# Cutting the tail's output stores differently, and issuing the very last piece from ScalarE's queue

## The chip, the cores and the metric

The kernel runs on one core of a Trainium2 chip. The metric is device time in microseconds (us), the median of several executions. Between two runs of one kernel the time varies by about 0.1 to 0.3%, so questions of half a per cent are asked here with five rounds, each beside a run of the kernel before on the same chip. A ratio given below is the mean time of one kernel's fast runs over the mean of the other's from the same rounds, so it is not quite the ratio of the quoted medians.

A few words used throughout. A *store* is a DMA from on-chip memory to HBM. *Issue* is the moment when a sequencer hands the store over. The store then runs on 16 DMA engines, each moving its own rows, one *packet* per row here. Each engine reports when its share has *landed*; the store is complete with the last of these reports.

## The reference

```python
batch, m, k, n = 16, 512, 1024, 768
return (np.matmul(x, weight) + bias + residual).astype(np.float32)
```

All inputs and the output are float32. The core reads about 62 MB and writes 25 MB.

## The kernel before

The 8192 rows are worked on as 64 tiles of 128 rows, grouped by J = 8 into super tiles (index S). One partition holds 8 consecutive rows, so a super tile's load or store moves long contiguous rows. A tile's matmuls go in two column chunks, 512 and 256 wide. All large transfers are issued from the sync queue:

```python
def store(S, j0=0, j1=J, n0=0, nl=N):
    K_(nc.sync.dma_start(
        out=out_d[S, :, j0:j1, n0:n0 + nl], in_=ro[S][:, j0:j1, n0:n0 + nl]
    ))
```

`K_` keeps the order of the program on each engine. `finish(t)` is the VectorE add that takes tile t's product out of PSUM and writes the result row, which the store then reads. The tail of the program:

```python
for t in range(HEAD, n_t):
    # ... cast, loads, matmuls, transposes, adds cut ...
    if S == n_s - 1 and j == 0:
        store(S - 1)                    # 3072 KB
    if S == n_s - 1 and j == J // 2:
        store(S, 0, J // 2)             # tiles 0-3: 1536 KB
    if S == n_s - 1 and j == J - 1:
        store(S, J // 2, j)             # tiles 4-6: 1152 KB
t, S = n_t - 1, n_s - 1
for b, (n0, nl) in enumerate(chunks):   # the last tile, chunk by chunk
    po[t] = psum_o(t + b)
    for i in range(len(steps)):
        mm(t, i, n0, nl)
    finish(t, n0, nl)
    store(S, J - 1, J, n0, nl)          # 256 KB, then 128 KB
```

## Time and profile before

The median was 211.06 us (210.88 to 211.19, 3 runs).

| what | value | read from |
|---|---|---|
| span | 209.1 us | page |
| TensorE (PE) busy | 96% | page, busy table |
| sync DMA queue | 97.8% of 16 engines' time | page, queue table |
| last VectorE add ends | 204.9 us | timeline |
| last store: issue to landing | 3.3 us | list of DMA issues |

First, lines of the page of the kernel before: DMA use in 40 slices of the span (tenths), and two DMA queues (packets, MB, share of 16 engines). The q8 packets are fetches of 16 KB of instructions.

```profile
DMA  6999999999999999999999999999999999999966
q1 hardware_dynamic: 5328, 87.03, 97.8%
q8 instruction: 10, 0.16, 0.3%
```

The engines move data nearly all the time. The tail in the timeline of the kernel before (start us, us, engine, line, operation), from 198 us on:

```profile
200.37 4.06 PE L104 MATMUL po<-w_sb,xt 128*128 128x512 bf16 x24
...
201.94 0.96 DVE L131 TENSOR_TENSOR ro<-po,ro 128x768 f32<-128x768 f32 x1 [0.68 <-PE po L104]
202.93 3.02 SPq L78 DMA_DIRECT2D out_dram<-ro  x3
203.67 1.23 DVE L131 TENSOR_TENSOR ro<-po,ro 128x512 f32<-128x512 f32 x2 [0.77 <-PE po L104]
```

PE ends at 204.4 and VectorE at 204.9. Nothing but stores and the closing barriers is left after that. The first of the three issues of the sync queue (the SPq line merges them) starts when tile 6's add is done. The list of DMA issues of the kernel before (size, us from issue to landing):

```profile
out_dram<-ro SPq DMA_DIRECT2D x1, 1536.0 KB, 10.4
out_dram<-ro SPq DMA_DIRECT2D x1, 1152.0 KB, 4.2
out_dram<-ro SPq DMA_DIRECT2D x1, 256.0 KB, 3.4
out_dram<-ro SPq DMA_DIRECT2D x1, 128.0 KB, 3.3
```

And the windows of the kernel before, 1 us each. Behind the engines' busy times come the granted clock, the DMA share and GB/s:

```profile
core 0: us, PE busy (x) PEld busy (x) DVE busy (x) ACT busy (x) POOL busy (x), PEclk, DMA share, GB/s
201.00:202.00 1.00, 1.00 (x8) 0.60 (x7) 0.32 (x2) 0.00 (x0) 0.00 (x0) 1.00 0.67 283
202.00:203.00 1.00, 1.00 (x7) 0.43 (x5) 0.90 (x1) 0.00 (x0) 0.00 (x0) 1.00 0.32 135
203.00:204.00 1.00, 1.00 (x9) 0.71 (x8) 0.33 (x1) 0.00 (x0) 0.00 (x0) 1.00 0.41 172
204.00:205.00 1.00, 0.43 (x4) 0.14 (x2) 0.78 (x2) 0.00 (x0) 0.00 (x0) 1.00 1.05 442
205.00:206.00 1.00, 0.00 (x0) 0.00 (x0) 0.00 (x0) 0.00 (x0) 0.00 (x0) 1.00 1.01 406
206.00:207.00 1.00, 0.00 (x0) 0.00 (x0) 0.00 (x0) 0.00 (x0) 0.00 (x0) 1.00 0.85 340
207.00:208.00 1.00, 0.00 (x0) 0.00 (x0) 0.00 (x0) 0.00 (x0) 0.00 (x0) 1.00 0.68 238
```

Between 201 and 204 the DMA share falls from 0.67 to 0.32 and 0.41: a hole. The 1152 KB store was issued only at 202.93, and its first packet starts at 203.75. This hole is what the change aims at.

These are the landings of each tail store (first, 14th and 16th of 16, us):

```
kernel before   issued   first    14th    16th
1536 KB         193.91  201.21  203.44  204.30
1152 KB         202.93  206.92  207.07  207.12
 256 KB         204.39  207.57  207.71  207.76
 128 KB         204.92  207.95  208.13  208.18
```

The engines finish the 1536 KB store up to 3.1 us apart. Toward the end of the hole two of them are still at work, and the other fourteen are idle.

### The profile page before, as it was taken

The page shows a single profiled execution, that of the slowest core. Times are in us where ns is not written, and L with a number is a line of the kernel's source. Part 1 is how long each engine was busy: PE and PEld are TensorE (multiplying, and loading weights), DVE is VectorE, ACT ScalarE, POOL GpSimd, SP SyncE. Part 2 cuts the span into 40 slices and gives each one's busy share as a digit, 9 for nine tenths or more (in the row PEclk, how much of TensorE's full clock was granted, in tenths as well). Part 3 has the DMA queues.
Part 4 walks back from the last instruction along what each step waited for, and adds up shares of the span by engine and source line. Part 5 has one row for each costly group of instructions (what it writes and reads, how often), then busy time and mean ns, then how long its engine had stood idle before and what let it go on. Part 6 is the DMA issues. An engine that isn't in the chain of part 4 may idle for free.

```text
span 209.1 us, 3149 instructions
## 1 busy us (share of the span) xinstructions
PE 201.1 (96%) x1274; PEld 130.8 (63%) x1299; DVE 105.0 (50%) x139; ACT 68.0 (33%) x68; POOL 115.6 (55%) x71
## 2 busy tenths in 40 slices
PE   7999999999899999999999999999999999999991
PEld 2556666666566666666666666666666666666660
DVE  0646564455354455445545544554554455446551
ACT  2544315520283054323423252440543234322000
POOL 2000197819936655999499802994069900799000
PEclk9999999999999999999999999999999999999999
DMA  6999999999999999999999999999999999999966
GB/s 229 428 422 432 430 421 438 443 456 407 404 476 420 409 432 412 443 428 434 437 415 459 415 414 447 437 426 418 428 431 443 445 412 421 432 442 423 414 287 273
DMA packets 5344, 87.23 MB, mean 417 GB/s; under 512 B 593, under 2 KB 721, under 8 KB 1618
## 3 DMA queue, kind: packets, MB, share of 16 engines
q1 hardware_dynamic: 5328, 87.03, 97.8%
q8 instruction: 10, 0.16, 0.3%
q14 instruction: 4, 0.03, 0.0%
q10 hardware_dynamic: 2, 0.00, 0.0%
HBM read 61.87 MB, written 25.17 MB: 416 GB/s over the span
## 4 chain that ended last, share of the span: by engine, by line
PE 70%; DMA 25%; issue 1%; ACT 1%; DVE 0%; POOL 0%; ACTq 0%; POOLq 0%
PE po L104 60%; DMA x_tile<-in_x_dram 23%; PE pt L95 10%; DMA tmp<-in_bias_dram 2%; ACT xb L87 1%; DVE ro L131 0%; POOL ident masks.py:197 0%; ACTq L87 0%; POOL tmp L135 0%; POOLq L262 0%
## 5 line engine op out<-in xcount | busy, mean ns | idle before, releaser
L104 PE MATMUL po<-w_sb,xt 128*128 128x512 bf16 (+1 forms) x999 | 175.4, 324 | 1.4
L104 PEld LDWEIGHTS <-xt 128*128 128x128 bf16 x1024 | 100.1, 98 | 59.5 <-DVE xt L99 0.5
L87 ACT CAST xb<-x_tile 128x1024 bf16<-128x1024 f32 x62 | 63.2, 1045 | 115.5 <-PE pt L95 63.2
L121 POOL TENSOR_TENSOR ro<-ro,bias_sb 128x768 f32<-128x768 f32 x40 | 71.2, 1816 | 34.6 <-DMA ro<-in_residual_dram 24.6
L99 DVE COPY xt<-pt 128x512 f32<-128x512 f32 x64 | 44.2, 692 | 88.3 <-PE pt L95 88.2
L121 POOL TENSOR_TENSOR ro<-ro,tmp 128x768 f32<-128x768 f32 x24 | 43.1, 1816 | 42.3 <-DMA ro<-in_residual_dram 25.0
L131 DVE TENSOR_TENSOR ro<-po,ro 128x768 f32<-128x768 f32 (+2 forms) x41 | 38.0, 930 | 2.9 <-PE po L104 2.8
L95 PE MATMUL pt<-ident,xb 128*128 128x128 f32 x256 | 38.6, 274 | 0.7 <-ACT xb L87 0.7
L95 PEld LDWEIGHTS pt<-ident,xb 128*128 128x128 f32 x256 | 30.1, 142 | 9.2 <-ACT xb L87 1.3
L129 DVE TENSOR_TENSOR tmp<-po,bias_sb 128x768 f32<-128x768 f32 x24 | 22.8, 949 | 0.4 <-PE po L104 0.4
L170 PE MATMUL po<-warm 128*128 128x512 bf16 x15 | 6.1, 579 | 1.2 <-DVE warm L156 1.2
L176 ACT CAST w_sb<-ro 128x768 bf16<-128x768 f32 x4 | 3.3, 832 | 4.0 <-DMA ro<-in_weight_dram 4.0
L170 PEld LDWEIGHTS <-warm 128*128 128x128 bf16 x15 | 1.9, 132 | 4.1 <-issue 2.8
L87 DVE CAST xb<-x_tile 128x1024 bf16<-128x1024 f32 x2 | 1.4, 694 | 5.1 <-DMA x_tile<-in_x_dram 5.1
L178 DVE CAST w_sb<-ro 128x768 bf16<-128x768 f32 x4 | 2.2, 556 | 2.2 <-DMA ro<-in_weight_dram 2.2
L161 ACT ACT_TABLE_LOAD x1 | 1.3, 1283 | 2.0 <-POOL ident masks.py:199 2.0
L190 PE MATMUL po<-tmp 128*128 128x512 f32 (+1 forms) x4 | 1.5, 486 | 0.0
L198 DVE COPY bias_sb<-po 128x768 f32<-128x768 f32 x1 | 1.0, 958 | 0.1
L190 PEld LDWEIGHTS po<-tmp 128*128 128x128 f32 x4 | 0.7, 190 | 0.5 <-issue 0.5
L135 POOL MEMSET tmp<- 128x768 f32 x1 | 0.7, 737 | 0.3 <-POOLq L262 0.3
L156 DVE MEMSET warm<- 128x256 uint32 x1 | 0.3, 272 | 0.9 <-PEq L262 0.9
masks.py:199 POOL TENSOR_SCALAR_AFFINE_SELECT ident<-ident 128x128 f32<-128x128 f32 x1 | 0.3, 292 | 0.1
(8 smaller groups left out, 1.0 us busy)
## 6 DMA issues: line engine op xcount, KB each, us to landing
x_tile<-in_x_dram SPq DMA_DIRECT2D x6, 4096.0 KB, 29.4
ro<-in_residual_dram SPq DMA_DIRECT2D x7, 3072.0 KB, 18.0
out_dram<-ro SPq DMA_DIRECT2D x7, 3072.0 KB, 24.9
x_tile<-in_x_dram SPq DMA_DIRECT2D x2, 2048.0 KB, 23.9
x_tile<-in_x_dram SPq DMA_DIRECT2D x3, 1024.0 KB, 8.7
ro<-in_weight_dram SPq DMA_DIRECT2D x4, 768.0 KB, 9.1
ro<-in_residual_dram SPq DMA_DIRECT2D x2, 1536.0 KB, 20.9
out_dram<-ro SPq DMA_DIRECT2D x1, 1536.0 KB, 10.4
```

The costliest lines, as they stand in the source:

```text
L87: K_(copy(out=xb[t], in_=x_sb[t // J][:, t % J, :]))
L95: K_(nc.tensor.transpose(out=pt[:, c, :], in_=pairs[:, c * P:(c + 1) * P], identity=ident))
L99: K_(nc.vector.tensor_copy(out=xt[t], in_=pt))
L104: K_(nc.tensor.matmul(po[t][:, n0:n0 + nl], lhsT=both[:, e, :], rhs=w_sb[:, c, e, n0:n0 + nl], start=(i == 0), stop=(i == len(steps) - 1),))
L121: K_(nc.gpsimd.tensor_add(out=r, in0=r, in1=tmp[t] if t < EARLY else bias_sb))
L129: K_(nc.vector.tensor_add(out=tmp[t], in0=p, in1=bias_sb))
L131: K_(nc.vector.tensor_add(out=row(t, n0, nl), in0=p, in1=row(t, n0, nl)))
L161: K_(nc.scalar.copy(out=warm_a, in_=warm_a))
L170: K_(nc.tensor.matmul(warm_ps[:, 0:512], lhsT=warm[:, 0:P], rhs=warm, start=True, stop=True))
L176: K_(nc.scalar.copy(out=w_sb[:, c, e, :], in_=w_st[:, c, e, :]))
L178: K_(nc.vector.tensor_copy(out=w_sb[:, c, e, :], in_=w_st[:, c, e, :]))
L190: K_(nc.tensor.matmul(bias_ps[:, n0:n0 + nl], lhsT=ones, rhs=bias_row[:, n0:n0 + nl], start=True, stop=True,))
```

## The change

Tiles 4 and 5 shall leave 3 us sooner, so that the hole fills; tile 6 follows alone. The very last piece goes out from ScalarE, which is idle by then, since the sync queue spends 1.02 us on that issue.

```diff
-    def store(S, j0=0, j1=J, n0=0, nl=N):
-        K_(nc.sync.dma_start(
+    def store(S, j0=0, j1=J, n0=0, nl=N, queue=nc.sync):
+        K_(queue.dma_start(
             out=out_d[S, :, j0:j1, n0:n0 + nl], in_=ro[S][:, j0:j1, n0:n0 + nl]
         ))
@@
+        if S == n_s - 1 and j == J - 2:
+            store(S, J // 2, j)
         if S == n_s - 1 and j == J - 1:
-            store(S, J // 2, j)
+            store(S, j - 1, j)
@@
         finish(t, n0, nl)
-        store(S, J - 1, J, n0, nl)
+        store(S, J - 1, J, n0, nl, nc.scalar if b else nc.sync)
```

## The prediction

> **What bounds it.** The page's busy table gives PE 96% of the 209.1 us span, its queue table the sync queue 97.8% of the time of 16 DMA engines. After the last matmul the transfers alone count: in the timeline of the tail PE ends at 204.4, the last VectorE add at 204.9, the last store is issued at 204.92 and lands at 208.2 (issue to landing 3.3 us); then barriers to 209.1. The change can touch only the 3.3 us between the last add and that landing.
>
> **What the change does.** No byte, matmul or add is added or removed. The 1152 KB store of tiles 4 to 6, issued at 202.93 after tile 6's add, becomes 768 KB issued after tile 5's add (ends 199.86, 3 us sooner) and 384 KB at 202.93: one more issue (0.33 us of an idle sequencer). The last 128 KB is issued by ScalarE, idle since about 190; its one earlier issue took 0.49 us, the sync queue's last one 1.02 us.
>
> **The tempting gain.** Issue to first packet took 0.83 us for the 1152 KB (202.93 to 203.75). In the window view the bandwidth falls to nearly zero around 203, because the earlier 1536 KB store has run out on most engines. With 768 KB queued early that hole fills: at about 430 GB/s the 1152 KB would be done at 205.3 rather than 206.65, and the last store could land near 206.8, 1.4 us sooner.
>
> **Why I do not expect it.** The Trainium skill, "DMA: Bandwidth & Descriptors", section "Why a DMA increments its semaphore by 16 and not by 1", says that a store runs on up to 16 engines that finish independently and that only all 16 mean landed. The trace agrees, and the engines are far apart: the 16 landings of the 1536 KB store spread from 201.21 to 204.30. Chaining the packet records into 16 engines, I read their last packets of that store at 200.8 to 203.83; 14 are done by 202.9, two at 203.76 and 203.83. The 1152 KB was ready at 203.75. So the two late engines had no hole: each ran without a gap to its last packet at about 207.7. With the change they still have 203.83 + 8 packets of 6144 B (estimate from that size at the start, 1.86 us) + 8 of 3072 B (estimate 0.95) + 8 of 2048 B (0.65, read) + 8 of 1024 B (0.38, read) = 207.7. The other 14 finish earlier and wait. Late engines' packets took the same 0.46 us per 12288 B when others were idle, so I expect no speed-up from that. The ScalarE queue saves issue time only (same page, "Issuing engines are not separate DMA queues"; no run here shows it yet): the last issue ended at 205.94, and the late engines reach its packets only at 207.3.
>
> Expected gain: 0 to 0.2 us.
>
> **Prediction.** 210.9 us, 8 times in 10 within 210.2 to 211.3. Faster by over 2%: 0.01; within 2%: 0.98; slower: 0.01.
>
> **What would show it.** Right: most of the 16 landings of the 768 KB and 384 KB come early, each store's last trails them by 2 to 3 us; DMA stays busy around 203 but thins out from 205.5 to 207.7; the last landing is again at 208.1 to 208.2; the last add still ends at 204.9.
>
> **What would make it wrong.** If the late engines' lag is not there in the new run (instruction fetches of 16 KB, 0.9 us each, may fall elsewhere), or they speed up alone, the end moves toward 206.8 and the time toward 209.7. If ScalarE's queue starts slowly (its first DMA took 4 us to its first packet, behind loads), the end could slip by up to 1 us.

## The result, and the profile after

The changed kernel took 211.13 us (median of 6, 210.96 to 211.40), the kernel before 211.01 in the same rounds. The ratio is 1.0005, with a 95% interval of 0.9992 to 1.0018: the same time. The profiled run: its span is 209.4 us.

The timeline and the issues of the changed kernel:

```profile
199.90 4.83 SPq L78 DMA_DIRECT2D out_dram<-ro  x3
...
203.67 1.23 DVE L131 TENSOR_TENSOR ro<-po,ro 128x512 f32<-128x512 f32 x2 [0.77 <-PE po L104]
204.98 0.38 ACTq L78 DMA_DIRECT2D out_dram<-ro  x1
```

```profile
out_dram<-ro SPq DMA_DIRECT2D x1, 768.0 KB, 6.5
out_dram<-ro SPq DMA_DIRECT2D x1, 384.0 KB, 4.4
out_dram<-ro SPq DMA_DIRECT2D x1, 256.0 KB, 3.6
out_dram<-ro ACTq DMA_DIRECT2D x1, 128.0 KB, 3.3
```

The 768 KB are issued at 199.90, as intended, and ScalarE's issue takes 0.38 us. Yet the last store still needs 3.3 us from issue to landing. The windows of the changed kernel:

```profile
201.00:202.00 1.00, 1.00 (x8) 0.60 (x7) 0.32 (x2) 0.00 (x0) 0.00 (x0) 1.00 0.97 412
202.00:203.00 1.00, 1.00 (x7) 0.42 (x5) 0.91 (x1) 0.00 (x0) 0.00 (x0) 1.00 0.85 356
203.00:204.00 1.00, 1.00 (x9) 0.71 (x8) 0.33 (x1) 0.00 (x0) 0.00 (x0) 1.00 0.77 320
204.00:205.00 1.00, 0.44 (x5) 0.15 (x2) 0.79 (x2) 0.00 (x0) 0.00 (x0) 1.00 0.87 353
205.00:206.00 1.00, 0.00 (x0) 0.00 (x0) 0.00 (x0) 0.00 (x0) 0.00 (x0) 1.00 0.89 343
206.00:207.00 1.00, 0.00 (x0) 0.00 (x0) 0.00 (x0) 0.00 (x0) 0.00 (x0) 1.00 0.46 166
207.00:208.00 1.00, 0.00 (x0) 0.00 (x0) 0.00 (x0) 0.00 (x0) 0.00 (x0) 1.00 0.11 41
```

The hole is filled: the share is 0.97, 0.85 and 0.77 where it was 0.67, 0.32 and 0.41. But the work does not end sooner. It thins out, to 0.46 and then 0.11, where before all engines stopped together. The landings say who is left:

```
changed kernel  issued   first    14th    16th
1536 KB         193.92  201.23  203.38  204.62
 768 KB         199.90  203.05  205.30  206.44
 384 KB         202.93  205.06  206.24  207.36
 256 KB         204.39  206.24  206.88  207.99
 128 KB         204.98  206.61  207.21  208.33   (the 15th: 208.10)
```

Fourteen engines have landed everything by 207.21, 0.9 us sooner than the 14th landing before. The last two land at 208.10 and 208.33, where the last of before was 208.18. The sync queue's waits at the end, between 198 and 210 us (what for: us in total, times, longest), first before, then after:

```profile
SPq L273 <- DMA out_dram<-ro: 2.1, 3, 1.2
```

```profile
SPq L275 <- DMA out_dram<-ro: 3.6, 1, 3.6
```

After the change the sync queue is done with its issues 1.2 us sooner (at 204.73, before at 205.95, by the SPq lines). It then waits that much longer, for an end that has not moved.

### The profile page after: what moved, and what is told of

Same layout as the page of the kernel before. It is cut to its first block, busy times and chain, and to the rows that moved or that the text cites. A ratio compares the mean times of both kernels' runs of the same rounds, so it can differ in the third digit from the quotient of the medians.

```text
span 209.4 us, 3151 instructions
## 1 busy us (share of the span) xinstructions
PE 200.2 (96%) x1274; PEld 130.5 (62%) x1299; DVE 105.0 (50%) x139; ACT 68.1 (33%) x68; POOL 115.6 (55%) x71
## 4 chain that ended last, share of the span: by engine, by line
PE 70%; DMA 25%; issue 1%; ACT 1%; DVE 0%; POOL 0%; ACTq 0%; POOLq 0%
PE po L104 60%; DMA x_tile<-in_x_dram 23%; PE pt L95 10%; DMA tmp<-in_bias_dram 2%; ACT xb L87 1%; DVE ro L131 0%; POOL ident masks.py:197 0%; ACTq L87 0%; POOL tmp L135 0%; POOLq L264 0%
## 5 line engine op out<-in xcount | busy, mean ns | idle before, releaser
L170 PE MATMUL po<-warm 128*128 128x512 bf16 x15 | 5.3, 520 | 1.2 <-DVE warm L156 1.2
```

What stands on the lines that cost most here:

```text
L170: K_(nc.tensor.matmul(warm_ps[:, 0:512], lhsT=warm[:, 0:P], rhs=warm, start=True, stop=True))
```

## The experiments

**The theory (late engines).** Loads and stores have kept the queue full for most of the run, and two engines lag behind the others. In the kernel before they come to the end of their backlog at 203.76 and 203.83, just when the 1152 KB becomes available (203.75): they never saw the hole. More work offered early only makes the other fourteen finish sooner.
**Rivals.** (a) The split gains something and ScalarE's queue loses it again. (b) The end is bound by fixed latencies after the last add, so nothing done to the queue can matter. (c) The backlog of all engines together hides the gain, not two late ones.

### The two halves of the change alone

The first run keeps only the split:

```diff
-        store(S, J - 1, J, n0, nl, nc.scalar if b else nc.sync)
+        store(S, J - 1, J, n0, nl)
```

> Only the split; the last piece stays on the sync queue. Late-engine theory: the two late DMA engines set the end whoever issues, so the time is that of before and after, within 0.3 us (210.8 to 211.4), and the last landing is again at 208.1 to 208.4. Rival (the split gains, ScalarE's queue loses it again): this one is faster than before by 0.5 us or more.

Measured: 211.27 us against 211.31 for before, ratio 0.9993 (0.9981 to 1.0005). In the profiled run, 14 of 16 landings of the last store were in by 207.42, the last two at 208.85 and 208.97. The sync queue's last issue took 0.33 us here, against 1.02 in the kernel before, so with the split there was little left for ScalarE's queue to save.

The second keeps only the queue (`store(S, J // 2, j)` restored, the split's two lines removed):

> Only the other queue; tiles 4 to 6 stay one store. Late-engine theory: same time within 0.3 us, landings of the last store within 0.3 us of each other as before, because the 1152 KB store starts when even the late engines are done. Rival (ScalarE's queue costs what the split gains): slower than before by 0.5 us or more.

Measured: 211.68 us, ratio 1.0016 (1.0000 to 1.0033). The landings of the last store lie between 208.27 and 208.75, further apart than the 0.3 us expected: one engine's share of the 1536 KB landed only at 205.1, and it still trailed the next by 0.3 us at the end. Rival (a) falls: by its interval the split alone gains at most 0.4 us, where 0.5 or more was asked for. Whether the other queue alone costs the 0.16% is at the edge of what these runs resolve (the interval allows 0 to 0.7 us).

### A level start for the tail

If lateness is the cause, the change must gain once the engines are level. This needs the backlog to run out before the tail's stores. It is done by not loading half of the last super tile's x; the data of an earlier super tile is used instead, so the result is wrong (four tiles), with all matmuls and stores unchanged.

```diff
-            if j0 == 0:
+            if S == n_s - 1:
+                x_sb[S], j0 = x_sb[S - X_BUFS], J // 2
+            elif j0 == 0:
                 x_sb[S] = ring(sb, "x_tile", S, X_BUFS, [P, J, K], FP32)
```

The same edit was made in the kernel before, in the changed kernel, and in the split alone.

> The kernel before with 2 MB less to load (the first half of the last super tile's x is not loaded; the previous contents are used, so four tiles are wrong on purpose). The queue then runs dry some 4 us earlier and all engines are idle before the tail's stores. Late-engine theory: same time as before within 0.4 us (210.6 to 211.4), because the 1152 KB store still starts at about 203.7 and ends at 206.6, and the last store lands at about 208.2. Rival (the tail is bound by queue backlog in total): faster by 1 us or more.

> The changed kernel with the same 2 MB less. Late-engine theory: with the engines level before the tail's stores, the gain that the change was meant for appears: last landing at 206.6 to 206.9, time 1.0 to 1.6 us below the light kernel before (209.4 to 210.1). Rival (the end is bound by fixed latencies after the last add, 3.3 us from issue to landing and then barriers): no difference from the light kernel before, within 0.3 us.

> The split alone on the light queue, the last piece on the sync queue. Late-engine theory: the split brings all of the gain; within 0.3 us of the light changed kernel. Rival (the sync queue's long last issue of 1.02 us matters once the engines are level): 0.4 to 0.7 us slower than the light changed kernel.

Measured, five executions each, beside 211.29 us for the kernel before:

| 2 MB less to load in | median, us | ratio to before (95%) |
|---|---|---|
| the kernel before | 211.23 | 0.9997 (0.9984 to 1.0011) |
| the changed kernel | 209.95 | 0.9935 (0.9923 to 0.9948) |
| the split alone | 209.86 | 0.9931 (0.9918 to 0.9945) |

One execution of the first row, the profiled one, took 763 us. It is left out of its ratio (it still counts in its median). Its trace shows TensorE slow throughout (a 128x512 matmul took 1104 ns on average, against 379 in the run below, with VectorE's adds at 948 ns in both); why is not known.

> The light kernel before once more, only because its first profiled execution took 763 us against 211.2 in the other four: a profile of an ordinary execution. Time 210.8 to 211.6; landings of the last store within 0.3 us of each other, the last at 208.0 to 208.4.

It took 211.19 us. The windows of this light kernel before, and then the last line of its list of DMA issues:

```profile
202.00:203.00 1.00, 1.00 (x6) 0.44 (x5) 0.78 (x1) 0.00 (x0) 0.00 (x0) 1.00 0.00 0
203.00:204.00 1.00, 1.00 (x8) 0.59 (x6) 0.23 (x2) 0.00 (x0) 0.00 (x0) 1.00 0.00 0
206.00:207.00 1.00, 0.00 (x0) 0.00 (x0) 0.00 (x0) 0.00 (x0) 0.00 (x0) 1.00 0.82 338
207.00:208.00 1.00, 0.00 (x0) 0.00 (x0) 0.00 (x0) 0.00 (x0) 0.00 (x0) 0.93 0.96 349
```

```profile
out_dram<-ro SPq DMA_DIRECT2D x1, 128.0 KB, 3.3
```

The same two views of the light changed kernel:

```profile
202.00:203.00 1.00, 1.00 (x6) 0.48 (x5) 0.95 (x1) 0.00 (x0) 0.00 (x0) 1.00 0.74 289
203.00:204.00 1.00, 1.00 (x9) 0.65 (x7) 0.23 (x2) 0.00 (x0) 0.00 (x0) 1.00 0.16 61
206.00:207.00 1.00, 0.00 (x0) 0.00 (x0) 0.00 (x0) 0.00 (x0) 0.00 (x0) 1.00 0.43 143
207.00:208.00 1.00, 0.00 (x0) 0.00 (x0) 0.00 (x0) 0.00 (x0) 0.00 (x0) 0.91 0.00 0
```

```profile
out_dram<-ro ACTq DMA_DIRECT2D x1, 128.0 KB, 1.9
```

And the last line of the list of the light split:

```profile
out_dram<-ro SPq DMA_DIRECT2D x1, 128.0 KB, 1.9
```

Both light kernels have all engines idle in the middle of the tail, so all 16 start level. The light kernel before has gained nothing from 2 MB less work: the hole has only become complete (share 0.00), and the last store still takes 3.3 us. In the light changed kernel the last store takes 1.9 us, and its landings lie between 206.71 and 206.95. This is the 1.3 us that the change was meant to bring (211.23 to 209.95). So the change works as intended once the backlog is gone. Rival (b) falls: the 3.3 us are not fixed. The lighter load takes the backlog from all sixteen engines, so this pair alone does not tell the two late engines from rival (c); the landings above and a comparison of four runs below do. The split brings all of it; with ScalarE's queue or the sync queue the last store takes 1.9 us. The sync queue's last issue, 1.02 us in the kernel before, takes 0.33 us in the light split, as it did in the split alone with the full load.

### Which engines are late

The Trainium skill ("DMA: Bandwidth & Descriptors", section "Why a DMA increments its semaphore by 16 and not by 1") states that a store uses the largest number of engines up to 16 that divides its row count, and the lowest-numbered ones. So a piece cut by partitions into row counts such as 88 (11 engines) can tell where the late ones are. The first attempt cut the last 128 KB into six stores (the edit is shortened here):

```diff
+for rows in (4, 8, 12, 14, 15, 75):
+    K_(nc.scalar.dma_start(out=out_d[S, p0:p0 + rows, ...], in_=ro[S][p0:p0 + rows, ...]))
+    p0 += rows
```

> The changed kernel with the last 128 KB cut by partitions into six stores of 4, 8, 12, 14, 15 and 75 rows, to learn how many engines each uses and whether the late ones are among them. Late-engine theory with the skill's rule for the number of engines: 4, 8, 12, 14, 15 and 15 landings, and in each store the landings of late engines trail the others by 1 to 2.5 us; the store in which the late landings first appear brackets the late engines' numbers. Rival (lateness belongs to the last rows written, not to an engine): all six land together at the end or one after the other in order of issue. Time 0 to 1 us longer than the changed kernel for five more issues.

It took 213.15 us, 2.0 us more than the changed kernel where at most 1 was expected, and its profile cannot place the late engines: more stores in flight made tile 6's store wait for a semaphore of one of the small ones (issued at 206.7, not 202.9), so the late engines had caught up by then. It does show the landings: 4, 8, 12, 14, 15 and 15, as the skill says of the number.

The next cut the 256 KB piece into 2 and 126 rows and the 128 KB into 8 and 120 (ScalarE's queue):

> A cleaner probe: in the changed kernel the 256 KB piece is cut by partitions into 2 and 126 rows, the last 128 KB into 8 and 120 rows. By the skill's rule for the number of engines (lowest-numbered k) these use 2, 14, 8 and 15 engines. Late-engine theory: the late landings, trailing by 1 to 2.5 us, appear only in the stores whose engines include the late ones; two of 16 are late, so the 14-engine store shows two late landings unless a late engine is number 14 or 15, and the 8-engine store shows none, one or two. Rival (lateness belongs to each store's last rows): every store shows its late landings. Time within 0.7 us of the changed kernel.

It took 211.45 us (211.22 for before). The 2-engine store landed at 205.7; the 14-engine store has one very late landing, at 208.22 against 207.4 for the one before it; the 15-engine store also has one (208.56 against 207.9). So one late engine is among numbers 2 to 13, counting from 0. The expectation of the next run takes the other for the sixteenth, since the 15-engine store has only one very late landing. The packet records show otherwise: the engine that finished tile 6's 384 KB last of all (landing 207.61) then moved eight packets of the 15-engine store, until 207.54, and none of the 14-engine store. By the rule it is number 14. Its landing at 207.9 is less late only because it had no share of the 256 KB. The 8-engine store, on ScalarE's own queue, had its last landing at 207.6 and says little: there its single packets may not have waited behind the sync queue's. The third cut therefore put everything on the sync queue, as 8 and 120, then 88 and 40 rows:

> To find the second late engine: the changed kernel with both pieces of the last tile on the sync queue, where an engine takes its packets in order, cut by partitions into 8 and 120 rows (256 KB piece), then 88 and 40 rows (128 KB piece), so 8, 15, 11 and 10 engines. The earlier cut showed one very late landing among 14 engines and one among 15, none among the first 2, so one late engine should be the sixteenth and the other one of numbers 2 to 13. Expected: one very late landing (2 us or more behind) in the 15-engine store; in the 8, 11 and 10-engine stores it appears if the engine's number is below 8, 11 and 10, and then in all larger ones. Rival (lateness follows rows, or is spread anew in each store): the four stores disagree with any single number. Time within 0.7 us of the changed kernel.

It took 211.03 us (211.37 for before, one run each). The 15-engine store had one very late landing, at 208.33, with the next at 207.73. The 8-, 11- and 10-engine stores had none so late: their last came at 206.78 (0.44 us after the second last), 208.00 and 208.17, the last two within 0.02 us of their second last. In the packet records the latest engine ends with its share of the 15-engine store (last packet 208.00) and has none of the 11-engine store, so it is one of 11 to 14. The second latest reads the same way, though its packets are harder to tell from others. With number 14 known from the cut before, the other late engine is then one of 11 to 13, if the two are the same in every build.

### Taking work off the late engines

The next expectation still says 15 where the records say 14. For its cut this makes no difference: both late engines have numbers above 10, so stores on 11 and 10 engines relieve them (the edit is shortened again; p0 starts at 0):

```diff
-            store(S, 0, J // 2)
+            for rows in (96, 22, 10):     # the control: (96, 16, 16)
+                K_(nc.sync.dma_start(out=out_d[S, p0:p0 + rows, 0:J // 2, :],
+                                     in_=ro[S][p0:p0 + rows, 0:J // 2, :]))
+                p0 += rows
```

> A version meant to beat both. The two cuts of the last tile placed the late engines among numbers 11 to 13 and at 15 (counting from 0). The changed kernel with the 1536 KB store of the last super tile's tiles 0 to 3 cut by partitions into 96, 22 and 10 rows: 16, 11 and 10 engines, so engines 0 to 9 move 9 rows of it, engine 10 moves 8, engines 11 to 15 move 6 rather than 8. Late-engine theory: the late engines' lag in the tail shrinks by 2 rows of 12288 B, 0.91 us, the others' grows by 0.46 us; the last landing comes 0.3 to 0.9 us sooner than in the changed kernel and the time is 210.2 to 210.8 where before has 211.1. Rival (the cut or its extra issues, not the relief, matter, or lateness is not tied to those engines): same time as before within 0.2 us.

> Control: the same cut into three stores, but 96, 16 and 16 rows, all on 16 engines, so each engine still moves 8 rows. Late-engine theory: no gain, time of the changed kernel within 0.25 us (210.9 to 211.4). Rival (any cut into three helps): as fast as the 96, 22 and 10 cut.

> The relieving cut (96, 22 and 10 rows) in the kernel before, where tiles 4 to 6 are one store issued at 202.9. Late-engine theory: the late engines finish earlier but then wait for that store's first packet at 203.75 like the others, so no gain: 211.0 to 211.4, last landing at 208.1 to 208.3. Rival (relief helps by itself, the split is not needed): 0.3 us or more faster than before.

| cut of the 1536 KB store | in | median, us | ratio to before (95%) |
|---|---|---|---|
| 96, 22, 10 (relief) | changed kernel | 212.46 | 1.0050 (1.0038 to 1.0062) |
| 96, 16, 16 (control) | changed kernel | 212.87 | 1.0076 (1.0062 to 1.0090) |
| 96, 22, 10 (relief) | kernel before | 210.99 | 0.9990 (0.9974 to 1.0006) |

The expected gain did not come, and the first two expectations failed: cutting this store by partitions is itself expensive. With 128 rows a packet of 12288 B took 460 ns at the median and 461 on average. In the relief cut the median is the same, but the average is 592 and the longest 1733 ns; in the control 560 and 1600. Eight packets per engine on average make that 8 x (592 - 461) ns = 1.05 us more work per engine, about the 1.1 us by which the relief version is slower than before (an average; what the latest engine lost follows below). The relief version is the faster of the two cut versions by 0.4 us, in the direction of the theory, but its packets were slower too, so this is no clean measurement of the relief. A likely reason is that the skill's "SBUF — State Buffer", section "Door 1: The DMA port swizzle", has groups of four partitions share one port. In a cut of 16 neighbouring rows over 16 engines several engines would read through one port. The slow packets are measured; that ports cause them was not tried.

The third row is the informative one. The same cut, with packets slow again (538 ns on average), costs the changed kernel 1.1 us and the kernel before nothing. There its last packet ended at 204.22 and its three parts had landed by 204.6. The next store's first packet started at 203.87, so the latest engine lost at most 0.35 us, and the 16 landings of that store lie within 0.28 us again. The hole that looked like waste is slack: it absorbs lateness.

The two slow cuts still serve to test the theory, for they made the latest engine later. From the packet records of the four profiled runs that have the split, the full load and an uncut last tile (us):

| run | last 1536 KB packet ends | very last packet ends | between them |
|---|---|---|---|
| changed kernel | 204.20 | 207.99 | 3.79 |
| the split alone | 204.85 | 208.64 | 3.79 |
| relief cut | 205.45 | 209.24 | 3.79 |
| control cut | 205.59 | 209.37 | 3.78 |

The latest engine's lateness differs by up to 1.4 us, and the end differs by just that. What lies between is that engine's own 32 packets without a gap (in the changed kernel 1.85 + 0.95 + 0.65 + 0.34 us for its eight of each size). This is what tells the late engines from rival (c).

### Where the lag comes from

This was read from the trace of the kernel before, not tried on the chip. Until 20 us the 16 landings of each transfer lie within 0.5 us. Then:

```
instruction fetch (16 KB) starts    next transfers' 16 landings, us behind the first
-                                   at  20.13: all within 0.49
 21.98                              at  23.89: fifteen within 0.43, one 1.47
 40.58                              at  44.67: fourteen within 0.43, then 1.48 1.57
 61.18                              at  61.77: thirteen within 0.34, then 1.39 1.48 1.57
174.91                              at 175.83: fifteen within 1.83, one 2.89
193.34                              at 197.59: fourteen within 2.08, then 2.94 3.05
```

Each of the ten fetches (the q8 line of the page) takes 0.99 to 1.11 us (the prediction put them at 0.9). After each of the first three there is one more engine that is 1 us later than it was; in between, the steps blur; after the last two, one engine and then two are nearly 3 us behind. They do not catch up as long as the queue does not run dry. The match in time and size is close, but no run changed the number of fetches, so it stays an inference.

## Why the prediction was right

- **Time.** 210.9 us was predicted (210.2 to 211.3), 211.13 was measured; the expected gain of 0 to 0.2 us was in fact none (ratio 1.0005).
- **The tempting gain that would not come.** The hole did fill, and the fourteen engines did land sooner. With level engines the gain is real: 1.3 us in the light kernels, against the 1.4 us named in the prediction. That it is lost in the real kernel to the late engines is shown by the landings and by the four runs in which the end follows the latest engine by 3.79 us; that it is not lost to fixed latencies or to ScalarE's queue, by the light pair and the two halves.
- **The sum for the late engines.** It gave 207.7 for their last packet. In the new run that was at 208.0. The term that was off is its start: the latest engine's last packet of the 1536 KB store ended at 204.20 instead of 203.83; the packets took what was estimated (6144 B: 234 ns, eight of them 1.87 us).
- **Partly luck.** In the trace that was read, the two late engines finished (203.76, 203.83) just as the hole closed (203.75). That start varies from run to run: in the profiled runs without a cut of the 1536 KB it was 203.83 in the kernel before, 204.68 with ScalarE's queue alone, 204.20 and 204.85 in the two with the split. By the same sum (an estimate), had the latest engine finished at 203.20 in the changed kernel, 1 us sooner, the last packet would have ended at 206.99, against 207.78 in the kernel before, and the change would have gained 0.8 us.
- **What would show it.** The late landings trail the first by 3.4, 2.3, 1.8 and 1.7 us in the four tail stores; 2 to 3 was said of the first two. The end of the transfers was 208.3, not 208.1 to 208.2. The last add ended at 204.9, as said.
- **ScalarE's queue.** Its slow start, named as a risk, did not happen: its first packet came about 0.9 us after issue. The gain from issuing elsewhere was nil, as the skill's section "Issuing engines are not separate DMA queues" has it; the light kernels now show this (209.95 against 209.86 us).
- **Not foreseen.** That a cut by partitions slows the packets. It spoiled the version that was to beat both kernels. No version that computes the right result was shown to be faster than the kernel before.

## What to carry to other kernels

A falling average bandwidth ahead of the end does not mean that time can be won there: look at the last of the 16 completions of each transfer, and ask whether that engine was ever idle. If the slowest engine has no gap, early issue and finer stores only help the others; first make the engines level, or take bytes off the slow one. When doing so, mind that cutting a store by partitions made packets slower here.

## What the Trainium skill lacked or had wrong

- "DMA: Bandwidth & Descriptors" says that the engines of one DMA finish independently, but not how far apart they can drift in a full queue: 0.5 us at 20 us of this run, 3.1 us at its end, with steps of about 1 us after five of the ten 16 KB instruction fetches (timing only; no run varied them).
- The same page advises against splitting a transfer into disjoint partition halves because they serialize. Neither it nor the SBUF page cited above has a figure for one store cut into such parts: here 96, 16 and 16 rows in place of 128 made the changed kernel 0.76% slower than the kernel before (uncut: 0.05%), with 12288 B packets at 560 ns on average in place of 461.
- Its rule for the number of engines held in every store cut here (2, 4, 8, 10, 11, 12, 14, 15 landings). Its fixed cost of about 2.0 us for a DMA, stated there for another path and without the time of the data, is more than was seen here: with level engines the last 128 KB took 1.9 us from issue to landing with the data, whose packets took 0.5 us (206.00 to 206.52). In the changed kernel it was 3.3 us because of the lag.
